# A decoder layer on one core: the first pooling group and a value projection change places with an attention block

## The chip, the cores and the metric

The kernel runs on one core of a Trainium2 chip. The metric is the device time of one launch in microseconds (us); the median of three runs is given. A profile is one further execution, recorded by the hardware profiler, whose span is measured from its first to its last instruction.

The engines are named as in the profile: PE (TensorE, matrix multiply; PEld is its weight load), DVE (VectorE), ACT (ScalarE), POOL (GpSimd) and SP (SyncE, which here only issues transfers).

## The reference

One decoder layer over 1024 tokens of width 1024, in float32. Cut to what matters here:

```python
z = h @ w_in                     # columns: [pool group 512 | q 512 | k 128 | v 128]
y_pool = pool_mixer(u_pool, w_pool, pool_scale)   # causal mean over 2, 4, 8, 16 tokens
                                                  # minus the token, then a 128x128 map
                                                  # per group of 128 channels, a scale per channel
y_attn = sliding_window_attention(q, k, v, sinks) # window 128, 8 query heads, 2 key heads,
                                                  # ALiBi bias, one sink per head
mix = concat(y_pool, y_attn) @ w_out
h = layer_norm(alpha * h + mix)
h = layer_norm(alpha * h + relu(h @ w_ff1)**2 @ w_ff2)
h = h + sigmoid(h @ w_gate + b) * (p @ w_ple)
```

## The kernel before

Each float32 operand is split into a high part, which ACT writes (`high`, L101), and a low part, which DVE computes as operand minus high part (`low`, L106). A product is then three matmuls on PE, high by high, high by low and low by high (`mm3`, L116 to L118).

The part that matters here is the first quarter of the kernel. The tokens are worked in two halves of 512 (`t` is 0 or 1). `z_tile(c, t)` loads one 128-column block of `w_in` (1024 rows), splits it, and issues 24 matmuls of 128x512 into one accumulator. Blocks 0 and 1 are the keys and values, 2 to 5 the queries, 6 to 9 the four pooling groups.

`attention(n)` (n is 0 to 7) treats 128 queries against 256 keys, for two key heads. For each key head it makes two score tiles `s` of 128x2x256 (L298, L299), adds bias and takes the row maximum on DVE (L302, one instruction for each of the two query heads of a tile, followed by a short read of its accumulator), exponentiates on ACT (L309), scales by the reciprocal on DVE (L313, L315), transposes on PE (L322), splits (L101, L106 on `pp`) and multiplies by the values (L327, L328) into `av`; L330 on ACT and L331 on DVE add its two halves.

`pool_group(gi, t, o)` takes the accumulator `o` of a pooling block: ACT copies it to a row (L358), POOL forms the window sums by doubling (L366) and mends the first tokens (L374, L375, first half only), DVE subtracts the token (L369), `tmp` takes the split result, three matmuls apply the 128x128 map into a new accumulator `y`, and ACT (L103) and DVE (L385) write the scaled and split result.

PSUM is shared out as follows. Accumulators `mm` have three buffers, score tiles `s` two, transposed tiles `pt` two, `av` one. `tmp` has one buffer. `out_left`, which multiplies the mixer's output by the left half of `w_out`, needs four accumulators and takes the fourth from the two `s` buffers:

```python
os = [acc_ps() for _ in range(3)]
os.append(ps.tile([P, HALF], F32, tag="s", bufs=2, name=nm("s")))
```

The order of the instructions on each engine is not the order of the program. The framework runs its own timeline model over the program (`schedule_with_timeline_sim=True`) and emits, on each engine, what the model finds ready, in program order where several are ready. A buffer is handed to the next tile of its kind once its last reader is done. So a change in the program's order moves instructions on all engines, up to where the two orders meet again. The weight loads of `z_tile` are issued on SP; a `st` buffer (two) is free for the next load when DVE has written the low part of the one before.

Before the change, `pooling(n)` keeps two pooling blocks projected and closes n groups; the sequence around the change is at L500 to L513.

Of the kernel before, what the change touches and what calls it, by code (L numbers as in the profile page):

```python
# [70 lines left out]
def layer(ctx, tc, xT, x, pT, w_in, w_pool, pscale, sinks, w_out, ln1, w1, w2, ln2, w_ple, w_gate, bgate, bias, rcount, out):  # L71
# [11 lines left out]
    def big(shape, dt=F32R):  # L83
        return sb.tile(shape, dt, tag="c", bufs=6, name=nm("c"))
# [7 lines left out]
    def stage(shape):  # L92
        return sb.tile(shape, F32, tag="st", bufs=2, name=nm("st"))
# [5 lines left out]
    def high(dst, src, scale=None):  # L99
        if scale is None:  # L100
            nc.scalar.copy(out=dst, in_=src)  # L101
        else:
            nc.scalar.mul(out=dst, in_=src, mul=scale)  # L103

    def low(eng, dst, src, hi):
        return eng.tensor_tensor(out=dst, in0=src, in1=hi.bitcast(F32), op=ALU.subtract)  # L106

    def load_split(dst_h, dst_l, src, shape, eng, st=None, queue=None):
        st = stage(shape) if st is None else st
        load = (queue or nc.sync).dma_start(out=st, in_=src)  # L110
        high(dst_h, st)
        low(eng, dst_l, st, dst_h)
        return load

    def mm3(o, ah, al, bh, bl, first, last, more=False):
        nc.tensor.matmul(o, ah, bh, start=first, stop=False, skip_group_check=more)  # L116
        nc.tensor.matmul(o, ah, bl, start=False, stop=False, skip_group_check=more)  # L117
        nc.tensor.matmul(o, al, bh, start=False, stop=last, skip_group_check=more)  # L118
# [30 lines left out]
    def keep(shape, dt=F32R):  # L149
        return pa.tile(shape, dt, tag="k", bufs=3, name=nm("k"))  # L150

    def tmp(shape, dt=F32):
        return pa.tile(shape, dt, tag="tmp", bufs=1, name=nm("tmp"))

    def row(shape, dt=F32):
        return pa.tile(shape, dt, tag="h", bufs=6, name=nm("h"))
# [14 lines left out]
    def acc_ps():  # L171
        return ps.tile([P, HALF], F32, tag="mm", bufs=3, name=nm("mm"))

    def tr_ps():
        return ps.tile([P, 4, P], F32, tag="pt", bufs=2, name=nm("pt"))
# [9 lines left out]
    def z_mm(o, w, t, k):  # L185
        xk = xs[t][k // 4]
        mm3(o, w[:, 0, k, :], w[:, 1, k, :], xk[:, 0, k % 4, :], xk[:, 1, k % 4, :], k == 0, k == NK - 1)
# [3 lines left out]
    def z_tile(c, t, home=None):  # L191
        w = (home or wt)([P, 2, NK, P])
        loads.append(load_split(w[:, 0], w[:, 1], w_in[c], [P, NK, P], nc.vector))
        o = acc_ps()
        for k in range(NK):
            z_mm(o, w, t, k)
        return o
# [45 lines left out]
    def values(t, o):  # L243
        if t == 0:
            VV[0] = keep([P, NT, 2, 2, HD])
        vt = row([P, HALF])
        copied = nc.scalar.copy(out=vt, in_=o)
        pv = tr_ps()
        for b in range(4):
            nc.tensor.transpose(pv[:, b, :], vt[:, b * P : (b + 1) * P], ident)  # L250
        v4 = pv.rearrange("p b (g d) -> p b g d", g=2)
        dst = VV[0][:, 4 * t : 4 * t + 4]
        for g in range(2):
            high(dst[:, :, g, 0, :], v4[:, :, g, :])
            low(nc.vector, dst[:, :, g, 1, :], v4[:, :, g, :], dst[:, :, g, 0, :])
        return copied
# [5 lines left out]
    def queries(t, half):  # L262
        for j in (2 * half, 2 * half + 1):
            o = first[2] if t == j == 0 else z_tile(2 + j, t, big if t == 0 and j == 1 else None)
            q = nat([P, 2, HALF], F32R)
            QQ[t][j] = q
            for i in range(2):
                r = slice(i * HD, (i + 1) * HD)
                sc = HD ** -0.5 / SLOPES[2 * j + i]
                high(q[0:HD, i, :], o[r, :], sc)  # L270
                nc.vector.scalar_tensor_tensor(
                    out=q[HD:P, i, :], in0=o[r, :], scalar=sc, in1=q[0:HD, i, :].bitcast(F32),
                    op0=ALU.mult, op1=ALU.subtract,
                )
# [69 lines left out]
    steps = [(gi, t) for t in range(2) for gi in (3, 2, 1, 0)]  # L344
    ahead = []

    def pooling(n):
        for _ in range(n):
            while steps and len(ahead) < 2:
                gi, t = steps.pop(0)  # L350
                ahead.append((gi, t, z_tile(6 + gi, t)))
            pool_group(*ahead.pop(0))

    def pool_group(gi, t, o):
        win = WINDOWS[gi]
        u = row([P, PAD + HALF])
        nc.gpsimd.tensor_copy(out=u[:, 0:PAD], in_=halo[:, gi, :])
        nc.scalar.copy(out=u[:, PAD:], in_=o)  # L358
        if t == 0:
            nc.gpsimd.tensor_copy(out=halo[:, gi, :], in_=u[:, HALF : HALF + PAD])  # L360
        sums = [row([P, PAD + HALF]) for _ in range(2)]
        cur, a, side = 1, u, 0
        while cur < win:
            d0 = 2 * cur - 1
            b = sums[side]
            nc.gpsimd.tensor_tensor(out=b[:, d0:], in0=a[:, d0:], in1=a[:, d0 - cur : PAD + HALF - cur], op=ALU.add)  # L366
            a, side, cur = b, 1 - side, 2 * cur
        dd = sums[side][:, PAD:]
        nc.vector.scalar_tensor_tensor(  # L369
            out=dd, in0=a[:, PAD:], scalar=1.0 / win, in1=u[:, PAD:], op0=ALU.mult, op1=ALU.subtract  # L370
        )
        if t == 0:
            f = win - 1
            nc.gpsimd.tensor_tensor(out=dd[:, 0:f], in0=a[:, PAD : PAD + f], in1=rc[:, 0:f], op=ALU.mult)  # L374
            nc.gpsimd.tensor_tensor(out=dd[:, 0:f], in0=dd[:, 0:f], in1=u[:, PAD : PAD + f], op=ALU.subtract)  # L375
        dT = tmp([P, 2, HALF], F32R)
        high(dT[:, 0], dd)
        low(nc.vector, dT[:, 1], dd, dT[:, 0])
        y = acc_ps()
        mm3(y, wp[:, 0, gi, :], wp[:, 1, gi, :], dT[:, 0], dT[:, 1], True, True)  # L380
        if mixP[t] is None:
            mixP[t] = big([P, 2, 4, HALF])
        m = mixP[t]
        high(m[:, 0, gi, :], y, psc[:, gi : gi + 1])
        nc.vector.scalar_tensor_tensor(  # L385
            out=m[:, 1, gi, :], in0=y, scalar=psc[:, gi : gi + 1], in1=m[:, 0, gi, :].bitcast(F32),
            op0=ALU.mult, op1=ALU.subtract,
        )
# [71 lines left out]
    def out_left(t, staging, eng, room=None):  # L460
        blocks = range(4 * t, 4 * t + 4)
        os = [acc_ps() for _ in range(3)]
        os.append(ps.tile([P, HALF], F32, tag="s", bufs=2, name=nm("s")))
        for k in range(NK):
            if k % 2 == 0:
                w = room[:, k // 2 - 2] if room is not None and k > 3 else wt([P, 2, 2, HALF])
                out_load(w, 0, k // 2, staging(), eng)
            for n in blocks:
                out_mm(os[n % 4], n, k, w)
        return os  # L470
# [29 lines left out]
    keys(1, z_tile(0, 1))  # L500
    attention(2)
    queries(1, 1)
    pooling(1)
    attention(3)
    values(1, z_tile(1, 1))
    pooling(1)
    attention(4)
    pooling(2)
    attention(5)
    pooling(2)  # L510
    attention(6)
    pooling(2)
    left = out_left(0, lambda: stage([P, 2, HALF]), nc.vector)  # L513
    with tc.issue_after(loads[-1].ins):
        residual_load(0)
# [639 lines left out]
```

## Time and profile before

| | |
|---|---|
| median of three runs | 984.94 us (984.05 to 985.39) |
| the profiled execution, its own time | 984.01 us |
| its span, first to last instruction | 982.2 us, granted TensorE clock 1.000 |
| PE busy in the span | 973.8 us of 982.2 |
| DVE, ACT, POOL busy | 750.4, 470.6, 129.5 us |

The profiled execution's own time is 1.8 us more than its span, and 0.93 us below the median of the runs. In the profile, "idle before" an instruction is the time in which its engine did nothing, and the arrow names what it waited for. In a timeline row stand the start, the duration, the engine, the line, the operation, the tile written and those read, and the shapes; rows of one group are merged, so that "x4" is four instructions one after another.

### The profile page before, as it was taken

The numbers are of one execution on the slowest core, as the hardware profiler recorded it, in microseconds if no ns is written. First come the engines' busy times: TensorE is split into PE (matmuls) and PEld (weight loads), VectorE is DVE, ScalarE is ACT, GpSimd is POOL, SyncE is SP. The second block draws the span as 40 slices with busy tenths as digits, with TensorE's granted clock in tenths as the row PEclk, the third lists the DMA queues.
The fourth block names the chain that finished last, engine by engine and source line by source line (L and its number), as shares of the span: only waits on it lengthen the run. The fifth ranks groups of instructions, "written<-read, shape, count | busy, mean of one in ns | idle before, by whom it ended". The sixth has DMA issues, their size and how long they took to land.

```text
span 982.2 us, 12301 instructions
## 1 busy us (share of the span) xinstructions
PE 973.8 (99%) x4474; PEld 809.3 (82%) x4474; DVE 750.4 (76%) x1188; ACT 470.6 (48%) x749; POOL 129.5 (13%) x185
## 2 busy tenths in 40 slices
PE   9999999999999999999999999999999999999998
PEld 7888887888888888888888888888888888878887
DVE  5798888895868876867547666888657699799895
ACT  5676666543475443434444344443434354554341
POOL 0013552020010000110000000100011111203210
PEclk9999999999999999999999999999999999999999
DMA  6512142623152544896264794675788866762741
GB/s 220 183 65 86 44 150 75 219 82 115 69 198 103 197 150 159 298 324 242 78 245 172 278 322 149 150 243 194 207 217 190 223 158 225 252 193 77 257 148 55
DMA packets 48188, 172.13 MB, mean 175 GB/s; under 512 B 6016, under 2 KB 7168, under 8 KB 45312
## 3 DMA queue, kind: packets, MB, share of 16 engines
q1 hardware_dynamic: 35584, 130.05, 38.6%
q0 software_dynamic: 10960, 36.71, 14.6%
q10 hardware_dynamic: 1584, 4.59, 1.2%
q8 instruction: 35, 0.57, 0.2%
q14 instruction: 25, 0.20, 0.1%
HBM read 138.82 MB, written 32.51 MB: 174 GB/s over the span
## 4 chain that ended last, share of the span: by engine, by line
PE 94%; DVE 2%; DMA 2%; issue 1%; ACT 1%; DVEq 0%
PE f L117 21%; PE f L118 21%; PE f L116 21%; PE mm L116 8%; PE mm L118 8%; PE mm L117 8%; DMA ws<-in_w_gate 2%; PE pt L322 1%; PE s L299 1%; PE s L298 1%; PE av L328 1%; PE av L327 1%; DVE w L106 0%; PE s L116 0%; ACT c L101 0%
## 5 line engine op out<-in xcount | busy, mean ns | idle before, releaser
L117 PE MATMUL f<-x,w 128*128 128x512 f32 x448 | 174.0, 389 | 0.4 <-DVE x L106 0.4
L118 PE MATMUL f<-x,w 128*128 128x512 f32 x448 | 173.9, 389 | 0.0
L116 PE MATMUL f<-c,ws 128*128 128x512 f32 (+1 forms) x420 | 162.5, 387 | 0.0
L117 PE MATMUL f<-c,ws 128*128 128x512 f32 (+1 forms) x420 | 162.5, 387 | 0.0
L118 PE MATMUL f<-c,ws 128*128 128x512 f32 (+1 forms) x420 | 161.3, 387 | 0.0
L116 PE MATMUL f<-x,w 128*128 128x512 f32 x448 | 147.1, 389 | 0.1
L101 ACT CAST w<-st 128x1024 fp32r<-128x1024 f32 (+2 forms) x66 | 65.6, 999 | 100.2 <-issue 57.9
L106 DVE TENSOR_TENSOR w<-st,w 128x1024 fp32r<-128x1024 f32 (+2 forms) x66 | 77.5, 1177 | 46.9 <-ACT w L101 46.8
L117 PEld LDWEIGHTS f<-x,w 128*128 128x128 f32 x448 | 84.1, 188 | 18.8 <-DVE x L106 1.1
L116 PEld LDWEIGHTS f<-x,w 128*128 128x128 f32 x448 | 84.0, 188 | 17.9 <-ACT x L101 0.5
L118 PEld LDWEIGHTS f<-x,w 128*128 128x128 f32 x448 | 84.1, 188 | 17.3
L118 PEld LDWEIGHTS f<-c,ws 128*128 128x128 f32 x420 | 78.9, 188 | 16.5 <-DVE ws L106 0.4
L117 PEld LDWEIGHTS f<-c,ws 128*128 128x128 f32 x420 | 78.9, 188 | 16.0
L116 PEld LDWEIGHTS f<-c,ws 128*128 128x128 f32 x420 | 78.9, 188 | 16.0
L106 DVE TENSOR_TENSOR x<-ws,x 128x1024 fp32r<-128x1024 f32 x54 | 65.8, 1219 | 1.5 <-ACT x L101 1.5
L101 ACT CAST ws<-w 128x512 fp32r<-128x512 f32 x60 | 36.9, 622 | 52.0 <-PE f L118 26.5
L106 DVE TENSOR_TENSOR ws<-w,ws 128x512 fp32r<-128x512 f32 x60 | 41.2, 690 | 25.3 <-ACT ws L101 24.6
L101 ACT CAST x<-ws 128x1024 fp32r<-128x1024 f32 x54 | 56.6, 1048 | 7.4 <-DMA ws<-gT 4.0
L101 ACT CAST ws<-st 128x512 fp32r<-128x512 f32 x48 | 29.8, 620 | 62.2 <-DVE st L121 30.8
L116 PE MATMUL mm<-c,w 128*128 128x512 f32 x144 | 56.4, 396 | 0.3 <-ACT w L101 0.3
L118 PE MATMUL mm<-c,w 128*128 128x512 f32 x144 | 56.6, 394 | 0.0
L117 PE MATMUL mm<-c,w 128*128 128x512 f32 x144 | 56.4, 393 | 0.0
(236 smaller groups left out, 1905.5 us busy)
## 6 DMA issues: line engine op xcount, KB each, us to landing
ws<-in_w SPq DMA_DIRECT2D x70, 512.0 KB, 3.8
w<-in_w SPq DMA_DIRECT2D x16, 1024.0 KB, 5.4
c<-fd SPq DMA_DIRECT2D x6, 2048.0 KB, 8.6
fd<-n POOLq DMA_DIRECT2D x20, 512.0 KB, 4.3
ws<-in_w POOLq DMA_DIRECT2D x20, 512.0 KB, 7.6
st<-in_w_in SPq DMA_DIRECT2D x17, 512.0 KB, 3.4
ws<-in_w_gate SPq DMA_DIRECT2D x16, 512.0 KB, 4.6
w<-in_w SPq DMA_DIRECT2D x10, 512.0 KB, 4.0
```

What stands on the lines that cost most here:

```text
L101: nc.scalar.copy(out=dst, in_=src)
L106: return eng.tensor_tensor(out=dst, in0=src, in1=hi.bitcast(F32), op=ALU.subtract)
L116: nc.tensor.matmul(o, ah, bh, start=first, stop=False, skip_group_check=more)
L117: nc.tensor.matmul(o, ah, bl, start=False, stop=False, skip_group_check=more)
L118: nc.tensor.matmul(o, al, bh, start=False, stop=last, skip_group_check=more)
L298: nc.tensor.matmul(s[:, i, dst], ql, kt[:, 0, g, kk : kk + kn], start=True, stop=False)
L299: nc.tensor.matmul(s[:, i, dst], ql, kt[:, 1, g, kk : kk + kn], start=False, stop=True)
L322: nc.tensor.transpose(pt[:, i, :], e[:, i, kb * P : (kb + 1) * P], ident)
L327: nc.tensor.matmul(av, VV[0][:, blk, g], pp[:, 0], start=(kb == lo), stop=False)
L328: nc.tensor.matmul(av, VV[0][:, blk, g], pp[:, 1], start=False, stop=(kb == 1))
```

## The change

The function `pooling` is replaced by `project`, which only projects the next pooling block; the groups are closed by explicit calls of `pool_group`. The sequence of projections and groups is the same as before from `attention(4)` on. In front of it two things change places: the first pooling group (window 16, first half of the tokens) was closed ahead of `attention(3)` and is closed after it, and the projection of the second half's values, `z_tile(1, 1)`, was behind that group and stands ahead of it, while the rest of `values` follows it.

```diff
-    def pooling(n):
-        for _ in range(n):
-            while steps and len(ahead) < 2:
-                gi, t = steps.pop(0)
-                ahead.append((gi, t, z_tile(6 + gi, t)))
-            pool_group(*ahead.pop(0))
+    def project():
+        gi, t = steps.pop(0)
+        ahead.append((gi, t, z_tile(6 + gi, t)))
...
     attention(2)
     queries(1, 1)
-    pooling(1)
+    project()
+    project()
     attention(3)
-    values(1, z_tile(1, 1))
-    pooling(1)
+    zv = z_tile(1, 1)
+    pool_group(*ahead.pop(0))
+    values(1, zv)
+    project()
+    pool_group(*ahead.pop(0))
     attention(4)
-    pooling(2)
+    project()
+    pool_group(*ahead.pop(0))
+    project()
+    pool_group(*ahead.pop(0))
...
```

No instruction of the computation is added or removed; lines below the function stand three lower in the changed file (L369 is L366 there, L385 is L382). The orders of the two kernels differ on PE from the middle of `attention(3)`'s scores to the start of the second half's `out_left`, and are the same before and after.

On PE, at the end of the scores of `attention(3)`, there stood in a row before (`pt` transposes of attention 2; `s_1001`, `s_1044` and `s_1051` the second, third and fourth score tile of attention 3; `mm_984` the first pooling group's map; `mm_1099` the values' projection):

```order
L322 MATMUL pt_823<-ident,e_786 128x128 x4
L299 MATMUL s_1001<-k_283,n_344 128x256
L298 MATMUL s_1044<-k_283,n_395 128x256
L299 MATMUL s_1044<-k_283,n_395 128x256
L298 MATMUL s_1044<-k_283,n_395 128x256
L299 MATMUL s_1044<-k_283,n_395 128x256
L298 MATMUL s_1051<-k_283,n_430 128x256
L299 MATMUL s_1051<-k_283,n_430 128x256
L298 MATMUL s_1051<-k_283,n_430 128x256
L299 MATMUL s_1051<-k_283,n_430 128x256
L116 MATMUL mm_984<-tmp_981,wp 128x512
L116 MATMUL mm_1099<-c_136,w_1094 128x512
```

and now, at the same place (`s_978` is the second score tile, `mm_1076` the values' projection):

```order
L322 MATMUL pt_823<-ident,e_786 128x128 x4
L299 MATMUL s_978<-k_283,n_344 128x256
L298 MATMUL s_978<-k_283,n_344 128x256
L299 MATMUL s_978<-k_283,n_344 128x256
L116 MATMUL mm_1076<-c_136,w_1071 128x512
L117 MATMUL mm_1076<-c_136,w_1071 128x512
```

The eleventh of those projection matmuls is the first row here; behind it comes the third score tile, `s_1021`, and then the projection again:

```order
L117 MATMUL mm_1076<-c_136,w_1071 128x512
L298 MATMUL s_1021<-k_283,n_395 128x256
L299 MATMUL s_1021<-k_283,n_395 128x256
L298 MATMUL s_1021<-k_283,n_395 128x256
L299 MATMUL s_1021<-k_283,n_395 128x256
L118 MATMUL mm_1076<-c_136,w_1071 128x512
```

Eleven matmuls of the values' projection now stand between the second and the third score tile, and thirteen more between the third and the fourth, which was directly behind the third.

On DVE, in the same stretch, the first pooling group's subtraction stood ahead of the weight split `w_1135`, and both between the two score tiles' maxima; before:

```order
L302 ISA e_992,sm_993<-s_994,nd,sink_sb 128x256
L302 ISA sm_993 128x1
L369 SCALAR_TENSOR_TENSOR h_972<-h_973,h_968 128x512
L106 TENSOR_TENSOR w_1135<-st_1136,w_1135 128x1024
L302 ISA e_992,sm_993<-s_1001,nd,sink_sb 128x256
```

and now:

```order
L302 ISA e_969,sm_970<-s_971,nd,sink_sb 128x256
L302 ISA sm_970 128x1
L106 TENSOR_TENSOR w_1135<-st_1136,w_1135 128x1024
L366 SCALAR_TENSOR_TENSOR h_1105<-h_1106,h_1101 128x512
L331 TENSOR_TENSOR y_735<-av_762,yl_783 64x512
L302 ISA e_969,sm_970<-s_978,nd,sink_sb 128x256
```

L369 (now L366) and `w_1135` have changed places, and L331 of attention 2 now stands ahead of the second tile's maxima too.

On DVE, ahead of the left half of the first `out_left` (its fourth accumulator, `s_1775` on PE, takes the buffer of the score tile `s_1659`, which the L302 rows at the end read), there stood before:

```order
L369 SCALAR_TENSOR_TENSOR h_1742<-h_1743,h_1739 128x512
L313 RECIPROCAL sm_1608<-sm_1608 128x4
L385 SCALAR_TENSOR_TENSOR c_1555<-mm_1551,psc,c_1555 128x512
L315 TENSOR_SCALAR e_1607<-e_1607,sm_1608 128x256 x4
L385 SCALAR_TENSOR_TENSOR c_1555<-mm_1600,psc,c_1555 128x512
L106 TENSOR_TENSOR tmp_1747<-h_1742,tmp_1747 128x512
L106 TENSOR_TENSOR w_1805<-st_1806,w_1805 128x1024
L302 ISA e_1657,sm_1658<-s_1659,nd,sink_sb 128x256
```

and now:

```order
L382 SCALAR_TENSOR_TENSOR c_1555<-mm_1551,psc,c_1555 128x512
L302 ISA e_1607,sm_1608<-s_1616,nd,sink_sb 128x256
L302 ISA sm_1608 128x1
L106 TENSOR_TENSOR tmp_1597<-h_1592,tmp_1597 128x512
L302 ISA e_1607,sm_1608<-s_1616,nd,sink_sb 128x256
L302 ISA sm_1608 128x1
L106 TENSOR_TENSOR w_1776<-st_1777,w_1776 128x1024
L302 ISA e_1657,sm_1658<-s_1659,nd,sink_sb 128x256
```

The maxima of `s_1659` now stand ahead of `h_1742`, the scaling of `e_1607`, the result of `mm_1600`, `tmp_1747` and `w_1805`, all of which come behind them; `w_1805`, the second quarter of `w_out`, has moved 13 rows further back, behind the maxima of the next score tile and the scaling of `e_1657`.

More of the change, by code (lines that the diff above doesn't have):

```diff
@@ L502, in layer @@
     queries(1, 1)
-    pooling(1)
+    project()
+    project()
     attention(3)
-    values(1, z_tile(1, 1))
-    pooling(1)
+    zv = z_tile(1, 1)
[3 more added lines that the diff above has]
+    pool_group(*ahead.pop(0))
     attention(4)
-    pooling(2)
+    project()
+    pool_group(*ahead.pop(0))
+    project()
+    pool_group(*ahead.pop(0))
     attention(5)
-    pooling(2)
+    project()
+    pool_group(*ahead.pop(0))
+    project()
+    pool_group(*ahead.pop(0))
     attention(6)
-    pooling(2)
+    project()
+    pool_group(*ahead.pop(0))
+    pool_group(*ahead.pop(0))
     left = out_left(0, lambda: stage([P, 2, HALF]), nc.vector)
```

## The prediction

> **What bounds the kernel now.** I read the page's busy shares first, then the chain that ended last, then the busy time by stage, PE's waits, and the timeline at each wait.
>
> ```profile
> PE 973.8 (99%) x4474; PEld 809.3 (82%) x4474; DVE 750.4 (76%) x1188; ACT 470.6 (48%) x749; POOL 129.5 (13%) x185
> PE 94%; DVE 2%; DMA 2%; issue 1%; ACT 1%; DVEq 0%
> ```
>
> The first row gives each engine's busy time, the second the shares of the chain. PE carries 94% of it; a change that adds no PE work can gain only PE's idle time. Where that lies (columns: stretch, its length, busy time of PE, PEld, DVE, ACT and POOL, granted clock, DMA share, GB/s):
>
> ```profile
> 5.00:75.00 70.00, 69.68 (x338) 58.47 (x338) 56.71 (x123) 47.43 (x100) 6.71 (x8) 1.00 0.45 152
> 75.00:130.00 55.00, 54.10 (x294) 46.17 (x293) 43.88 (x107) 37.63 (x85) 24.35 (x36) 1.00 0.28 98
> 130.00:180.00 50.00, 48.79 (x253) 40.76 (x252) 43.90 (x105) 34.17 (x82) 18.31 (x21) 1.00 0.29 95
> 180.00:260.00 80.00, 80.00 (x376) 66.58 (x375) 61.74 (x121) 33.03 (x46) 10.32 (x9) 1.00 0.36 122
> 700.00:875.00 175.00, 174.51 (x768) 143.25 (x766) 136.95 (x156) 78.48 (x82) 23.16 (x32) 1.00 0.79 210
> 875.00:982.20 107.20, 103.11 (x482) 86.42 (x482) 91.24 (x149) 38.24 (x51) 16.99 (x29) 1.00 0.41 137
> ```
>
> The change reorders instructions between about 90 and 212 us. There PE is idle 0.90 us in one stretch and 1.21 us in another; the last stretch's 4.1 us are the output's tail behind the last matmul, which nothing here touches. PE's waits name the two:
>
> ```profile
> PE s L116 <- DVE sm L302: 1.2, 1, 1.2
> PE s L298 <- DVE sm L302: 0.9, 1, 0.9
> PE f L117 <- DVE x L106: 0.4, 1, 0.4
> ```
>
> Both waits are for a score buffer: PE may not write the next tile into one of the two `s` buffers until DVE's L302 has read the old one. They lie here (start, duration, engine, operation; idle time in brackets):
>
> ```profile
> 92.35 0.28 PE L298 MATMUL s<-k,n 128*128 128x256 f32 x1
> 92.47 0.28 PE L299 MATMUL s<-k,n 128*128 128x256 f32 x1
> 92.70 0.28 PE L299 MATMUL s<-k,n 128*128 128x256 f32 x1
> 93.88 0.39 PE L298 MATMUL s<-k,n 128*128 128x256 f32 x1 [0.90 <-DVE sm L302]
> 155.85 0.50 PE L117 MATMUL mm<-tmp,wp 128*128 128x512 f32 x1
> 156.18 0.40 PE L118 MATMUL mm<-tmp,wp 128*128 128x512 f32 x1
> 157.79 0.50 PE L116 MATMUL s<-w,c 128*128 128x512 f32 x1 [1.21 <-DVE sm L302]
> ```
>
> Starts are the better measure, since matmuls overlap. Score matmuls follow each other at 0.12 us (92.35 to 92.47), so the first wait costs 93.88 - 92.70 - 0.12 = 1.06 us. The pitch of 128x512 matmuls comes from a run of 18:
>
> ```profile
> 94.74 0.39 PE L116 MATMUL mm<-c,w 128*128 128x512 f32 x1
> 98.59 0.39 PE L118 MATMUL mm<-c,w 128*128 128x512 f32 x1
> ```
>
> 17 steps in 3.85 us, 0.227 us each; the second wait costs 157.79 - 156.18 - 0.23 = 1.38 us. What DVE did meanwhile:
>
> ```profile
> 91.19 0.69 DVE L369 SCALAR_TENSOR_TENSOR h<-h,h 128x512 f32<-128x512 f32 x1
> 91.79 1.22 DVE L106 TENSOR_TENSOR w<-st,w 128x1024 fp32r<-128x1024 f32 x1
> 92.93 0.48 DVE L302 CUSTOM_DVE_ANT_0 e<-s,nd,sink_sb 128x256 f32<-128x256 f32 x1
> 93.73 0.68 DVE L331 TENSOR_TENSOR y<-av,yl 64x512 f32<-64x512 f32 x1
> 151.19 0.68 DVE L369 SCALAR_TENSOR_TENSOR h<-h,h 128x512 f32<-128x512 f32 x1
> 151.89 0.75 DVE L385 SCALAR_TENSOR_TENSOR c<-mm,psc,c 128x512 fp32r<-128x512 f32 x1
> 152.56 1.41 DVE L315 TENSOR_SCALAR e<-e,sm 128x256 f32<-128x256 f32 x4
> 153.89 0.74 DVE L385 SCALAR_TENSOR_TENSOR c<-mm,psc,c 128x512 fp32r<-128x512 f32 x1
> 154.55 1.25 DVE L106 TENSOR_TENSOR tmp<-h,tmp 128x512 fp32r<-128x512 f32 x1
> 155.72 1.21 DVE L106 TENSOR_TENSOR w<-st,w 128x1024 fp32r<-128x1024 f32 x1
> 156.85 0.47 DVE L302 CUSTOM_DVE_ANT_0 e<-s,nd,sink_sb 128x256 f32<-128x256 f32 x1
> ```
>
> In both cases DVE works off pooling and weight pieces that stand ahead of the maxima PE waits for. That order is what moves.
>
> **The change, part by part.** Nothing is added or removed: the moved group's POOL adds, its ACT copy and casts, its DVE pieces and its three matmuls are the same, and PE's work is the same to the instruction. So the sum has only waits in it.
>
> *First wait.* PE finishes the second score tile at about 92.3 us as before. DVE still has a weight split (1.14 from start to start), L369 (0.60), and now L331 (0.68) ahead of that tile's maxima, and reads them by 91.2 + 2.4 + 0.8 = 94.4 us. PE does not ask then: 11 matmuls, the third tile (into the first tile's buffer, read by 91.2) and 13 more stand ahead of the fourth tile, 24 x 0.227 + 0.46 = 5.9 us, which it reaches at 98.2. The wait goes with 3.8 us to spare: -1.06 us. What is delayed is the chain behind the third tile, whose softmax starts 2.5 us later; its transposes stand behind all of attention 3's scores and 24 matmuls in both orders, so I put that at nothing.
>
> *Second wait.* Before, the buffer was free at about 157.65 (156.85 and two maxima at 0.4). Now h_1742 with a reciprocal, the scaling, one L385, tmp_1747 and w_1805 stand behind these maxima: by the starts above 0.70 + 1.33 + 0.66 + 1.17 + 1.13 = 5.0 us less ahead of them. So the buffer is free at 152.7 even if DVE reclaims no idle time. PE asked at 156.18 + 0.23 = 156.41; now it asks 1.06 us earlier for the first wait, and some 0.45 earlier because three matmuls of a pooling map went behind and one of attention came ahead: 154.9. The wait goes with 2.2 us to spare: -1.38 us.
>
> *What is late next.* w_1805, the second quarter of `w_out`. Behind it before, and ahead of it now, are four maxima, L331, two `pp` splits and one scaling of four, about 1.6 + 0.7 + 1.2 + 1.1 = 4.6 us; before it was written by 156.85, so by 161.5 if DVE ran as solidly as it did. PE needs it about 2.44 us earlier than it would, behind 16 rows that now come ahead of it (four of attention 0.9, eight transposes 0.9, four scores 0.46): I get 159.3. So this step costs between 0 and 2.2 us. DVE's idle stretches ahead of it say how much it can reclaim:
>
> ```profile
> 121.44 1.52 DVE L106 TENSOR_TENSOR w<-st,w 128x1024 fp32r<-128x1024 f32 x1 [0.48 <-ACT w L101]
> 129.44 0.48 DVE L302 CUSTOM_DVE_ANT_0 e<-s,nd,sink_sb 128x256 f32<-128x256 f32 x1 [1.99 <-PE pt L322]
> 137.01 0.69 DVE L106 TENSOR_TENSOR tmp<-h,tmp 128x512 fp32r<-128x512 f32 x1 [0.74 <-ACT tmp L101]
> 145.67 0.69 DVE L106 TENSOR_TENSOR tmp<-h,tmp 128x512 fp32r<-128x512 f32 x1 [0.76 <-ACT tmp L101]
> ```
>
> They sum to 3.97 us, most of it waiting for PE, which is now earlier. Following DVE's new order row by row with these durations, I find w_1805 written at about 157.7, 1.6 us ahead of need. I take 0 and keep 2.2 as the other end.
>
> *The rest of the stretch.* Walking PE's, DVE's, ACT's and POOL's new orders the same way, the tightest other places have 1.3 to 2 us to spare (the fifth pooling group's `tmp`, the scaling of attention 5). On SP the `w_in` loads keep their order; four rows of `w_out` and of x change places behind the left half. Two rows for that and for what comes later:
>
> ```profile
> ACT c L101 <- DMA st<-in_w_out: 4.3, 4, 1.6
> 829.47 1.06 ACT L101 CAST x<-ws 128x1024 fp32r<-128x1024 f32 x1 [3.47 <-PE f L118]
> ```
>
> ACT already waits for these `w_out` loads, four times, 1.6 us at most, and PE does not: its matmuls of the left half cover it. A load late by as much again would take that cover; price 0, at most 1.6 us. From the second `out_left` on the orders are equal and PE is solid to 869 us, so an earlier PE stays earlier. The 0.4 us wait of `f` there ends a chain of casts and loads that starts with the second row, which waits for a matmul; it moves along.
>
> One row speaks of DVE against POOL:
>
> ```profile
> 138.78 3.80 POOL L366 TENSOR_TENSOR h<-h 128x527 f32<-128x527 f32 x2 [1.02 <-ACT h L358]
> 141.85 2.46 DVE L315 TENSOR_SCALAR e<-e,sm 128x256 f32<-128x256 f32 x4
> 162.32 1.14 DVE L315 TENSOR_SCALAR e<-e,sm 128x256 f32<-128x256 f32 x4
> ```
>
> Beside POOL's adds the scaling took 2.46 us, without them 1.14, and two adds took 3.80. A collision costs DVE 1.3 us. The same number of adds and scalings meet in the same stretch; I price a change in their meetings from -1.3 to +1.3 us on DVE, value 0, and nothing on PE while 1.5 us are to spare. The Trainium skill ("SBUF — State Buffer", Who interferes with whom) has it that the two engines share one pair of ports as an exclusive lock, so that the later one blocks for a whole instruction; these rows agree in kind. By that rule alone the moved group's adds could hold DVE once more at each scaling they now meet, and the time would be that of the first rival below.
>
> *Sum.* -1.06 - 1.38 = -2.44 us. Against the profiled execution: 984.01 - 2.44 = 981.6; the median of the runs was 0.93 above it, so 984.94 - 2.44 = 982.5 us.
>
> **The rivals.** 0.2% is 2.0 us, about what a measurement of this kernel can tell from no change.
>
> *A part comes back.* The first wait goes, but DVE, which is busy 43.9 of 50 us between 130 and 180, is late with w_1805 or with one scaling because of one more collision: 1.3 us of 2.44 returned, 983.8. For it speak the solid DVE rows from 146 to 158; against it the 3.97 us idle.
>
> *Nothing gained.* The model placed the old order without seeing the two waits, so it can place new ones as large: w_1805's full 2.2 us gives 984.7. Against it: in my walk each place has over 1 us to spare.
>
> *Slower.* The left half's fourth accumulator holds one of the two `s` buffers from its first matmul to the end of the left half. Before, three of attention 7's four score tiles had to share the other buffer in that time, and the fourth came after; now all four come within it. Each then waits for two maxima of the one before. If DVE is over 4 us behind PE there (my walk has it 4 us ahead at the second tile), each pays about what the second wait paid: 4 x 1.38 = 5.5 us, less 2.44 gained, +3.1 or 988.0.
>
> **How the numbers follow.** Forecast as summed 0.54; a part back 0.25; nothing gained 0.11; slower 0.10. The predicted time is the first's, 982.5. Its own range is 981.7 to 983.3 (the bounds of small waits, and 0.7 us by which runs differ). The range goes on to the second and third cases: 981.5 to 985.3. For faster by over 0.2% the time must be under 982.97, so the first case falls there mostly, and a little to the other side: faster 0.50, within 0.2% 0.40, slower 0.10.
>
> **What would show it.** In the new profile PE should have no idle row of 0.9 before an L298 near 93 us, the third score tile should start near 94.8, and no L116 on `s` should wait near 155. PE idle in the stretch from 75 to 180 should be under 0.5 us instead of 2.1, busy time of PE the same, and the span 979.8. A wait of PE for DVE's `w` L106 near 159 would show the first rival or the second by its size; several waits for L302 between 157 and 175 the last. I would be wrong altogether if DVE's order lets a piece I took as early, such as `tmp`, hold PE where before it did not.

## The result, and the profile after

The changed kernel takes 982.76 us (median of 12 runs, 981.70 to 983.47) beside 984.75 us of the kernel before (12 runs, 983.59 to 986.25): a ratio of 0.9979, interval 0.9970 to 0.9987, or 2.0 us less. The profiled execution of it took 982.35 us with a span of 980.6. Its page, busy shares and chain:

```profile
PE 974.0 (99%) x4474; PEld 808.8 (82%) x4474; DVE 752.7 (77%) x1188; ACT 470.5 (48%) x749; POOL 126.5 (13%) x185
PE 90%; DVE 6%; DMA 2%; issue 1%; ACT 1%; ACTq 0%; DVEq 0%
```

PE's work is the same. DVE's share of the chain rose from 2% to 6%, but that says little by itself: a second profile of the old order (values_behind_group below) has 5%. What belongs to the change is a piece from 138.4 to 161.4 us, where the chain, followed back from a new wait, leaves PE and runs along DVE and ACT. The stretches and PE's waits:

```profile
75.00:130.00 55.00, 55.00 (x298) 46.91 (x297) 47.40 (x113) 38.71 (x89) 24.09 (x37) 1.00 0.25 89
130.00:180.00 50.00, 49.31 (x256) 40.89 (x255) 45.37 (x108) 35.34 (x84) 18.87 (x20) 1.00 0.34 117
```

```profile
PE s L117 <- DVE w L106: 0.5, 1, 0.5
PE av L328 <- DVE pp L106: 0.2, 1, 0.2
```

PE's idle time from 75 to 180 us fell from 2.11 to 0.69 us. Both waits for L302 are gone from the list, and two small ones for DVE's pieces have come. At the place of the first wait (timeline; the last matmul of the second score tile, the first of the third and of the fourth):

```profile
91.78 0.28 PE L299 MATMUL s<-k,n 128*128 128x256 f32 x1
...
94.42 0.28 PE L298 MATMUL s<-k,n 128*128 128x256 f32 x1
...
98.09 0.28 PE L298 MATMUL s<-k,n 128*128 128x256 f32 x1
```

Neither tile has idle time in front. At the place of the second, the fourth accumulator starts at the pitch of 0.23 us:

```profile
154.08 0.39 PE L118 MATMUL mm<-c,w 128*128 128x512 f32 x1
154.31 0.39 PE L116 MATMUL s<-w,c 128*128 128x512 f32 x1
```

What came instead lies 4 us later:

```profile
158.41 0.40 PE L116 MATMUL s<-w,c 128*128 128x512 f32 x1
159.34 0.50 PE L117 MATMUL s<-w,c 128*128 128x512 f32 x1 [0.53 <-DVE w L106]
...
160.75 0.47 PE L327 MATMUL av<-pp,k 128*128 128x512 f32 x1
161.38 0.50 PE L328 MATMUL av<-pp,k 128*128 128x512 f32 x1 [0.16 <-DVE pp L106]
```

From start to start PE lost 159.34 - 158.41 - 0.23 = 0.70 us waiting for the low part of `w_1805`, and 161.38 - 160.75 - 0.23 = 0.40 us for the low part of a `pp`. DVE and POOL at that time:

```profile
148.18 1.50 DVE L106 TENSOR_TENSOR w<-st,w 128x1024 fp32r<-128x1024 f32 x1
...
152.88 1.12 DVE L315 TENSOR_SCALAR e<-e,sm 128x256 f32<-128x256 f32 x4
...
156.19 1.96 DVE L315 TENSOR_SCALAR e<-e,sm 128x256 f32<-128x256 f32 x4
158.07 1.21 DVE L106 TENSOR_TENSOR w<-st,w 128x1024 fp32r<-128x1024 f32 x1
```

```profile
156.15 1.07 POOL L363 TENSOR_TENSOR h<-h 128x527 f32<-128x527 f32 x1 [4.34 <-DVE sm L313]
```

The scaling ahead of `w_1805` took 1.96 us beside POOL's add and 1.12 three microseconds earlier, without one.

**A finer measure than the run time.** From the eight transposes of attention 1 at 63 us to the first transposes into `av` at 233 us lies all that the change moves. The rows that bound it, of the kernel before and of the changed one:

```profile
63.10 1.03 PE L322 MATMUL pt<-ident,e 128*128 128x128 f32 x8
...
234.52 0.60 PE L444 MATMUL av<-ident,n 128*128 128x128 f32 x4
```

```profile
62.66 1.03 PE L322 MATMUL pt<-ident,e 128*128 128x128 f32 x8
...
232.79 0.60 PE L441 MATMUL av<-ident,n 128*128 128x128 f32 x4
```

That is 171.42 us before and 170.13 after: 1.29 us less, of 1.6 in the span. The same two rows of every profile taken in this study:

| kernel | start | stretch | rest of the span |
|---|---|---|---|
| before | 63.10 | 171.42 | 747.68 |
| values_behind_group (the order of before) | 64.01 | 171.46 | 747.23 |
| values_ahead_only | 62.83 | 171.79 | 747.78 |
| changed kernel | 62.66 | 170.13 | 747.81 |
| after_again (unaltered) | 63.51 | 170.15 | 746.94 |
| double_add | 62.83 | 170.71 | 747.76 |
| sum_on_dve | 63.29 | 169.92 | 747.19 |
| window2_direct | 63.04 | 169.33 | 747.63 |
| weights_first_window2 | 62.64 | 169.34 | 747.32 |
| weights_first | 63.12 | 169.01 | 748.27 |
| weights_first_again (unaltered) | 63.73 | 169.02 | 746.35 |
| no_sums | 63.05 | 168.59 | 746.36 |

Three orders were profiled twice, and their stretches repeat to 0.01, 0.02 and 0.04 us, while the start scatters over 1.4 us and the rest over 1.9 us whatever the kernel. The scatter of the runs is that of the start and the rest. So below the stretch carries the verdicts, and the ratio (to runs of the kernel before that were made beside each experiment) is given with it.

### The profile page after: what moved, and what is told of

The parts are those of the page before. It is cut to its first block, busy times and chain, and to the rows that moved or that the text cites. A ratio compares the mean times of both kernels' runs of the same rounds, so it can differ in the third digit from the quotient of the medians.

```text
span 980.6 us, 12293 instructions
## 1 busy us (share of the span) xinstructions
PE 974.0 (99%) x4474; PEld 808.8 (82%) x4474; DVE 752.7 (77%) x1188; ACT 470.5 (48%) x749; POOL 126.5 (13%) x185
## 4 chain that ended last, share of the span: by engine, by line
PE 90%; DVE 6%; DMA 2%; issue 1%; ACT 1%; ACTq 0%; DVEq 0%
PE f L117 21%; PE f L118 21%; PE f L116 20%; PE mm L116 8%; PE mm L117 8%; PE mm L118 8%; DMA ws<-in_w_gate 1%; DVE w L106 1%; PE pt L322 1%; DVE x L106 1%; PE s L299 1%; PE s L298 1%; PE av L328 1%; DVE pre L121 1%; PE av L327 1%
## 5 line engine op out<-in xcount | busy, mean ns | idle before, releaser
L118 PE MATMUL f<-c,ws 128*128 128x512 f32 (+1 forms) x420 | 161.4, 387 | 0.0
L118 PEld LDWEIGHTS f<-c,ws 128*128 128x128 f32 x420 | 78.9, 188 | 16.3 <-DVE ws L106 0.4
```

## The experiments

**One half of the change alone.** In values_behind_group the projection is moved and the group stays:

```diff
     project()
     project()
-    attention(3)
-    zv = z_tile(1, 1)
     pool_group(*ahead.pop(0))
+    zv = z_tile(1, 1)
+    attention(3)
     values(1, zv)
```

> One half of the change alone: the projection of the second half's values stands ahead of attention 3, but the first pooling group stays in its old place ahead of it. The scheduler gives every engine the rows of the kernel before, in the same order, so this is a second look at that program. Theory (both waits belong to that order): the ratio is 1.000 within 0.0007, and the profile shows both waits for a score buffer again, about 0.9 us before an L298 near 93 us and 1.2 us before an L116 on s near 157.8. Rival (part of what the two profiles differ by is the start of that one execution, where the changed kernel's rows stood 0.45 us earlier already at 63 us, ahead of any moved row): this profile stands nearer to the changed kernel's at 63 us, by up to 0.45 us.

983.9 us, ratio 0.9998 (0.9989 to 1.0007). Both waits are there again, to 0.01 us (idle 0.90 and 1.21 in the kernel before):

```profile
94.78 0.39 PE L298 MATMUL s<-k,n 128*128 128x256 f32 x1 [0.89 <-DVE sm L302]
...
158.72 0.51 PE L116 MATMUL s<-w,c 128*128 128x512 f32 x1 [1.21 <-DVE sm L302]
```

So the waits belong to the order and not to an execution. The rival on the start isn't borne out in its direction: the transposes stood at 64.01, 0.9 us later than before, not earlier. But it shows that the changed profile's lead of 0.44 us at that row is within what the same program does by itself. Half of the change is no change: the scheduler gives the old order back on every engine, so this run is a second look at the kernel before and no test of the projection alone.

In values_ahead_only the projection comes ahead of the group, and both ahead of attention 3:

```diff
     project()
     project()
-    attention(3)
     zv = z_tile(1, 1)
     pool_group(*ahead.pop(0))
+    attention(3)
     values(1, zv)
```

> The other way to make half of the change: the projection of the values stands ahead of the first pooling group, and both stay ahead of attention 3. Here all 24 of its matmuls come before attention 3's scores, and on DVE w_1805 stands behind the two maxima of s_1659, as in the changed kernel, but also behind pp_1488 and pp_1498. Theory (each wait goes when DVE's pieces ahead of the maxima go): no wait of about 1 us near 93 us, and the second wait shrinks from 1.38 by 1.13 (w_1805) less 0.65 (pp_1488), to about 0.9; so 1.06 + 0.5 = 1.6 us less than the kernel before, 983.2 us, ratio 0.9984. Rival (the moved group does it, its DVE piece and its three matmuls behind attention 3): both waits stay, ratio 1.000.

984.04 us, ratio 1.0001 (0.9992 to 1.0010), stretch 171.79: nothing gained. The theory had the old waits right and the time wrong: both are gone, even the 0.9 us that it had left of the second. In their place PE waits for the first half of a pooling `tmp`, which ACT casts late, and three shorter times. Its list of waits, and the largest in the timeline:

```profile
PE mm L116 <- ACT tmp L101: 0.9, 1, 0.9
...
PE s L298 <- DVE sm L302: 0.4, 2, 0.2
PE av L327 <- DVE y L331: 0.2, 1, 0.2
```

```profile
160.19 0.40 PE L118 MATMUL s<-w,c 128*128 128x512 f32 x1
161.50 0.50 PE L116 MATMUL mm<-tmp,wp 128*128 128x512 f32 x1 [0.91 <-ACT tmp L101]
```

161.50 - 160.19 - 0.23 = 1.08 us. My sum had ended at the waits that I knew, and priced at nothing what is late next. That is the step which failed in the prediction too.

**Is it POOL's add that makes w_1805 late?** First the add taken off POOL, then doubled. sum_on_dve:

```diff
-            nc.gpsimd.tensor_tensor(out=b[:, d0:], ...)
+            (nc.vector if t == 1 and gi == 0 else nc.gpsimd).tensor_tensor(out=b[:, d0:], ...)
```

> The changed kernel with the one window sum of the last pooling group (window 2, second half) added on DVE and not on POOL. PE's order is the same up to well behind 159 us; on DVE the sum stands between the scaling of attention 6 and w_1805. In the changed kernel POOL's add at 156.15 (1.07 us) lies beside that scaling, which takes 1.96 us and not the 1.12 of one alone, and w_1805 is written so late that PE waits 0.70 us for it and 0.40 for pp. Theory (POOL holds DVE up): the scaling takes 1.1 to 1.3 us; w_1805 comes 0.84 earlier for that and 0.6 later for the sum, so PE's wait for it is 0.4 to 0.5 us; time 982.0 to 982.7. Rival (DVE is late by the order and amount of its own work, the scaling is long for another reason): the scaling still takes about 1.9 us, w_1805 comes 0.6 later, PE's wait for it grows to 1.3 us, time 983.3.

981.43 us, less than both figures expected; ratio 0.9973 (0.9961 to 0.9984), stretch 169.92. The waits decide here. On DVE:

```profile
156.81 1.14 DVE L315 TENSOR_SCALAR e<-e,sm 128x256 f32<-128x256 f32 x4
157.87 0.70 DVE L363 TENSOR_TENSOR h<-h 128x527 f32<-128x527 f32 x1
```

On PE:

```profile
159.05 0.40 PE L116 MATMUL s<-w,c 128*128 128x512 f32 x1
159.76 0.51 PE L117 MATMUL s<-w,c 128*128 128x512 f32 x1 [0.31 <-DVE w L106]
```

The scaling is back to 1.14, and the wait is 0.71 - 0.23 = 0.48 us, as the theory had it and not the rival's 1.3. The stretch gained only 0.21 us, since the sum now stands on DVE ahead of `pp` too, for which PE waits 161.80 - 161.02 - 0.23 = 0.55 us:

```profile
161.02 0.39 PE L327 MATMUL av<-pp,k 128*128 128x512 f32 x1
161.80 0.50 PE L328 MATMUL av<-pp,k 128*128 128x512 f32 x1 [0.38 <-DVE pp L106]
```

double_add:

```diff
-            nc.gpsimd.tensor_tensor(out=b[:, d0:], ...)
+            for _ in range(2 if (t, gi) == (1, 0) else 1): nc.gpsimd.tensor_tensor(out=b[:, d0:], ...)
```

> The changed kernel with that one window sum done twice on POOL (the same values again). On DVE the rows up to w_1805 keep their order; behind it the last group's pieces come later, and on PE its map does. Theory (POOL holds DVE up): the second add of about 1.07 us lies beside the end of the scaling and w_1805, which together take 0.5 to 1.1 us longer; PE's wait for w_1805 grows from 0.70 to between 1.2 and 1.8 us, time 983.3 to 983.9. Rival (POOL's adds cost DVE nothing there): scaling and w_1805 take 1.96 and 1.21 us as in the changed kernel, PE's wait stays at 0.70, time 982.8.

983.1 us, between the theory's 983.3 and the rival's 982.8; ratio 0.9989 (0.9980 to 0.9998), stretch 170.71. On DVE, and then on PE:

```profile
156.36 2.84 DVE L315 TENSOR_SCALAR e<-e,sm 128x256 f32<-128x256 f32 x4
159.12 1.21 DVE L106 TENSOR_TENSOR w<-st,w 128x1024 fp32r<-128x1024 f32 x1
```

```profile
158.59 0.40 PE L116 MATMUL s<-w,c 128*128 128x512 f32 x1
160.38 0.50 PE L117 MATMUL s<-w,c 128*128 128x512 f32 x1 [1.40 <-DVE w L106]
```

The wait is 1.79 - 0.23 = 1.56 us. So with no, one and two adds the same scaling takes 1.14, 1.96 and 2.84 us, and PE waits for `w_1805` 0.48 (with the sum of 0.6 us on DVE in between), 0.70 and 1.56 us. POOL's add is shown to be a cause.

**The changed kernel once more.**

> The changed kernel once more, unaltered, to see how far its own runs and a second profile agree. The profiles so far, taken from the first transposes of attention 1 (63 us) to the first transposes into av at 233 us, give it 171.42 - 170.13 = 1.29 us less than before in that stretch, and nothing later. Theory (that stretch is the whole effect): a ratio between 0.9980 and 0.9990, and 170.1 us within 0.1 for the stretch. Rival (the first comparison's 2.0 us are right and part of the gain lies outside it): 0.9975 to 0.9980.

981.34 us, ratio 0.9982 (0.9974 to 0.9991), stretch 170.15. This agrees with the theory, but the interval reaches past the rival's figures too. The stretch repeats to 0.02 us. Whether some more of the gain lies outside it stays open: both comparisons show about 2 us, and the rest of the span, 747.81 and 746.94 in this order, 747.68 and 747.23 in the old one, scatters too much to tell.

**Without the add and without a sum.** window2_direct uses that a mean of two less the token is half the difference to the one before:

```diff
+        half = (gi, t) == (0, 1)
+        if half:
+            nc.gpsimd.tensor_scalar(out=u[:, 0:PAD], in0=halo[:, gi, :], scalar1=0.5, scalar2=None, op0=ALU.mult)
+            nc.scalar.mul(out=u[:, PAD:], in_=o, mul=0.5)
...
-        while cur < win:
+        while cur < win and not half:
...
+        if half:
+            add(dd, u[:, PAD - 1 : PAD + HALF - 1], u[:, PAD:], ALU.subtract)
```

> The changed kernel with the last pooling group's window of 2 formed without a sum: ACT halves the row as it copies it, and DVE's one subtraction takes the token from its predecessor, so POOL's 1.07 us add is gone and DVE has no instruction more. PE's order is the same; on DVE the subtraction (0.6 us) comes ahead of w_1805 instead of behind it. Theory (POOL's add holds the scaling up by 0.82 us): scaling 1.12 to 1.14 us; w_1805 0.82 earlier less 0.6, PE's wait for it about 0.5 instead of 0.70; everything behind it on DVE 0.8 earlier, so the wait of 0.40 for pp goes; the stretch from 63 to 233 us 169.5, ratio 0.9982 of before. Rival (the wait for pp comes from PE being earlier, not from DVE): it stays at 0.4 and the stretch is 169.9.

981.68 us, ratio 0.9982 (0.9973 to 0.9991), stretch 169.33 (169.5 expected). PE:

```profile
158.79 0.40 PE L116 MATMUL s<-w,c 128*128 128x512 f32 x1
159.49 0.50 PE L117 MATMUL s<-w,c 128*128 128x512 f32 x1 [0.30 <-DVE w L106]
```

The scaling took 1.15 us, the wait for `w_1805` is 0.47 us, and that for `pp` is gone: it was DVE's lateness too.

**The order of the pieces.** weights_first loads and splits the first two quarters of `w_out` ahead of the last group (`out_weights` does for one quarter what stood in `out_left`, which takes the two as they are):

```diff
     pool_group(*ahead.pop(0))
+    early = [out_weights(k, lambda: stage([P, 2, HALF]), nc.vector) for k in (0, 2)]
     pool_group(*ahead.pop(0))
-    left = out_left(0, lambda: stage([P, 2, HALF]), nc.vector)
+    left = out_left(0, lambda: stage([P, 2, HALF]), nc.vector, None, early)
```

> The changed kernel with the load and split of the first two quarters of w_out written ahead of the last pooling group in the program. On PE the fourth pp matmul and the second four transposes come ahead of a run of weights' matmuls; on DVE w_1805 keeps its place, and the two pp splits come ahead of the last group's subtraction instead of behind it. POOL's add stays. Theory (each wait is DVE's rows ahead of the piece waited for): the scaling still takes 1.96 us and the wait for w_1805 stays at 0.70; the pp pieces come 0.6 us earlier, so the wait of 0.40 for them goes, if nothing waits for the later subtraction; stretch from 63 to 233 us about 169.7, ratio 0.9984. Rival (the order of the program sets DVE's lateness as a whole): the wait for w_1805 goes too, 169.0.

981.4 us, ratio 0.9981 (0.9973 to 0.9990), stretch 169.01. The rival's figure, by the theory's mechanism: I had looked at PE's and DVE's order and not at ACT's. ACT casts `w_1805` ahead of the row's copy, so POOL's add starts 0.90 us behind the scaling, where it started 0.04 ahead of it in the changed kernel, and holds none of its four instructions:

```profile
155.89 1.04 ACT L101 CAST w<-st 128x1024 fp32r<-128x1024 f32 x1
156.83 0.57 ACT L355 COPY h<-mm 128x512 f32<-128x512 f32 x1
```

```profile
156.64 1.14 DVE L315 TENSOR_SCALAR e<-e,sm 128x256 f32<-128x256 f32 x4
157.70 1.22 DVE L106 TENSOR_TENSOR w<-st,w 128x1024 fp32r<-128x1024 f32 x1
```

```profile
157.54 2.30 POOL L363 TENSOR_TENSOR h<-h 128x527 f32<-128x527 f32 x1 [5.29 <-ACT h L355]
```

Now it is POOL that is held up: its add takes 2.30 us, 1.07 and the 1.22 of DVE's split, which lost nothing. PE waits for neither `w_1805` nor the first `pp`.

With both edits:

> Both edits together: no POOL add in the last group, and the split w_1805 ahead of that group's subtraction on DVE. Theory (POOL's add is what made w_1805 late; without it the forecast's own walk holds): w_1805 is written 0.82 us earlier than in the changed kernel and PE does not wait for it (0.70 gone); pp comes 0.8 earlier while PE asks 0.7 earlier, so 0.3 us of 0.40 stay at most; the stretch from 63 to 233 us is 169.1 (171.42 of before less the 2.44 forecast makes 169.0), ratio 0.9976 of before. Rival (DVE is late for its amount of work): w_1805 is still waited for, 0.3 us or more, and the stretch is 169.6 or more.

981.09 us, ratio 0.9975 (0.9966 to 0.9984), stretch 169.34:

```profile
158.40 0.40 PE L116 MATMUL s<-w,c 128*128 128x512 f32 x1
158.63 0.39 PE L117 MATMUL s<-w,c 128*128 128x512 f32 x1
...
159.90 0.47 PE L327 MATMUL av<-pp,k 128*128 128x512 f32 x1
160.53 0.50 PE L328 MATMUL av<-pp,k 128*128 128x512 f32 x1 [0.16 <-DVE pp L106]
```

No wait for `w_1805`, as the theory says; but the 0.40 for `pp` stayed whole, where I expected 0.3 at most, because that split stands behind the group's subtraction on DVE; in weights_first, where the first `pp` split stands ahead of it, PE does not wait. The stretch missed 169.1 by that.

**The shortest one again.**

> The kernel with the first two quarters of w_out loaded and split ahead of the last pooling group, once more and unaltered, since its stretch from 63 to 233 us (169.01) was the shortest seen, though the last expectation had it wrong: ACT casts w_1805 ahead of the row's copy there, so POOL's add starts 0.7 us later, behind the scaling, which took 1.14 us. Theory (the stretch repeats, the rest of the span does not): 169.0 within 0.05, a ratio of 0.9975 to 0.9983 of before. Rival (the stretch was a chance of that execution): 169.5 or more.

980.79 us, ratio 0.9972 (0.9963 to 0.9981), stretch 169.02. It repeats. This version is 1.1 us shorter in the stretch than the changed kernel; the run times (0.9981 and 0.9972 beside 0.9979 and 0.9982) don't separate the two.

**All window sums left out.**

> The changed kernel without any of POOL's window sums: each pooling group takes the row itself where the sum stood, so 20 adds of POOL are left out and the rest stays; the engines' orders shift between 90 and 212 us. DVE has the same instructions. In the changed kernel DVE is busy 47.40 and 45.37 us in the stretches from 75 to 130 and from 130 to 180 us. Theory (POOL's adds hold DVE up): by the excess of its rows over the time of the same instruction alone, 5.0 us in the scalings and about 2 in the rest, DVE's busy time there falls from 92.8 to between 85 and 88 us, and no scaling of four takes over 1.5 us but beside another POOL instruction. Rival (the long rows have another cause): it stays within 1 us of 92.8.

One run, 979.8 us; stretch 168.59. PE is idle nowhere from 75 to 180 us here. DVE is busy 87.5 us in that time, within the 85 to 88 expected, where it was 92.8; but work has also moved out of the window (40 scalings lie in it instead of 44, and from 180 to 260 us DVE is busy 64.21 us where it was 60.40). Over the whole kernel, with the same 1188 instructions, DVE's time falls only from 752.7 to 750.2 us:

```profile
PE 972.2 (99%) x4474; PEld 808.7 (83%) x4474; DVE 750.2 (77%) x1188; ACT 469.7 (48%) x749; POOL 103.0 (11%) x165
```

The scalings, in the changed kernel and here (groups of DVE from 75 to 180 us, busy and mean of one):

```profile
L315 DVE TENSOR_SCALAR e<-e,sm 128x256 f32<-128x256 f32 x44 | 17.5, 456 | 0.2
```

```profile
L315 DVE TENSOR_SCALAR e<-e,sm 128x256 f32<-128x256 f32 x40 | 11.7, 350 | 0.2
```

350 ns each, where they were 456: no long scaling is left. Over the whole kernel the 56 scalings of this shape take 16.3 us here and 21.0 in the changed kernel. But the order has moved too, and sums are not all that holds DVE up. The scaling at 143.22 us of the changed kernel (2.19 us) lay beside a split of `c` on POOL (143.70, 1.29 us). Here three splits of `tmp` on DVE, 0.67 to 0.69 us alone, take 1.43 to 1.73 us beside such splits; the first of them:

```profile
87.59 1.73 DVE L106 TENSOR_TENSOR tmp<-h,tmp 128x512 fp32r<-128x512 f32 x1
```

```profile
87.48 1.29 POOL L106 TENSOR_TENSOR c<-y,c 128x512 fp32r<-128x512 f32 x1 [1.25 <-ACT c L101]
```

So the long scalings come from meetings with POOL's instructions, its sums and its splits of `c`. The 2 us that the theory expected from the rest of DVE's rows did not come.

## Why the prediction was right, and where it was wrong

*First wait, -1.06 us:* right. The third score tile started at 94.42 (forecast 94.8) and the fourth at 98.09 (98.2), without idle time.

*Second wait, -1.38 us:* right. PE asked at 154.31 (154.9) and got the buffer at once.

*What is late next, 0:* wrong, and this is the step that failed. I named the place, the tile and the bound (0 to 2.2 us), and took the lower end from my walk along DVE: `w_1805` written at 157.7, 1.6 us ahead of need. It was written at 158.07 + 1.21 = 159.28 and cost 0.70 us, and the `pp` behind it 0.40 more. Of the 1.6 us between walk and trace, 0.84 is the scaling at 156.19 (1.96 for 1.12), and 0.3 the split at 148.18 (1.50 for 1.21). The rest of some 0.5 I did not trace, and it is more like 0.9, since the changed profile already stands 0.44 us earlier at 63 us. The prediction had counted the scaling among the rows ahead of `w_1805` at 1.1 us, the time of one alone. It also called the 3.97 us of idle time mostly waits for PE; only 1.99 of them are, and the others are waits for ACT.

*POOL against DVE, -1.3 to +1.3 on DVE, 0 on PE:* wrong in size and in consequence. "The same number of adds and scalings meet" did not hold: DVE's busy time rose by 2.3 us for the same 1188 instructions (750.4 before and 750.5 in values_behind_group, 752.7 and 752.6 in the two profiles of the changed kernel). The scalings more than account for it, with 18.1 us over the whole kernel before and 21.0 after. Before, the longest row of four took 2.46 us and two took 1.41; now the rows at 143.22 and 156.19 take 2.19 and 1.96, and two more are long:

```profile
102.75 3.00 DVE L315 TENSOR_SCALAR e<-e,sm 128x256 f32<-128x256 f32 x4
132.45 2.26 DVE L315 TENSOR_SCALAR e<-e,sm 128x256 f32<-128x256 f32 x4
```

The one at 156.19 is shown to reach PE; the one at 143.22 lies on the chain too, and what it costs was not measured. I let the term cost PE nothing "while 1.5 us are to spare", which the same walk had found. The two terms were not independent: one collision took half of the spare time of the other.

*The rest:* right as far as can be seen. No other wait appeared between 75 and 260 us, and the rest of the span did not shorten by more than it scatters (747.68 and 747.23 in the old order, 747.81 and 746.94 in the new).

*Sum:* 2.44 forecast; in the stretch 2.44 - 0.70 - 0.40 = 1.34 worked out from the waits, 1.29 measured. So what happened is the first rival: the two waits went, and "one more collision" took back 1.1 us, of the 1.3 that I gave it. The two terms of the forecast hold where nothing comes behind them: in weights_first, where PE waits for neither `w_1805` nor the first `pp`, the stretch is 171.42 - 169.01 = 2.41 us shorter than before. The median came out at 982.76, 0.26 from the forecast and under the line of 982.97, because the first comparison shows 2.0 us less, of which the stretch accounts for 1.29; a second one gave 0.9982. The difference lies inside the intervals. So the forecast's closeness is luck: its sum is nearly twice the gain that the stretch shows, and the 0.7 us that bring the median near it are located nowhere. Of the signs that I listed, PE idle from 75 to 180 us is 0.69 (under 0.5 forecast), the span 980.6 (979.8), and the wait for `w` near 159 named the first rival, as the list said it would.

*The two other rivals* did not occur here. But "nothing gained" is what the other half of the change did (values_ahead_only): new waits as large as the old.

## What to carry to other kernels

When a wait is removed, walk on to the piece that is late next, and walk it twice: once with the durations of rows that stood alone and once with those that met a neighbour; price what the second walk loses, even where the first one has more to spare than one collision costs (here 1.6 us beside 0.84). Read the orders of all engines, ACT's and POOL's too, since one cast that changes places with a copy on ACT can decide whether DVE and POOL meet. Where a change acts within one stretch, measure from a fixed row ahead of it to a fixed row behind it: here that repeats to 0.04 us, while the run times of the same program scatter over 2 us and more.

## What the runs showed of the hardware

How an add on POOL and an instruction on DVE share time was known in kind from the profile before, but not which of the two pays. Where POOL's add came as a scaling began (156.15 against 156.19) the scaling waited: 1.14, 1.96 and 2.84 us with no, one and two adds, 0.82 and 0.88 us for each of about 1.07. Each add holds one of the four instructions: with one add the first took 1.17 us and the other three 0.34 each. Where DVE was already in a row of instructions (weights_first: the scaling from 156.64 to 157.78, the split from 157.70), DVE lost nothing, and the add, whose row begins at 157.54, took 2.30 us. A split on POOL does the same as an add: the scaling at 143.22 and the `tmp` split at 87.59 were held beside one.

The Trainium skill ("SBUF — State Buffer", Who interferes with whom) says that a DVE instruction in a mode that uses two ports, which it says `tensor_scalar` can enter, contends with POOL for a shared pair of ports, that whoever issues first gets the pair for the whole instruction, and that the other fully blocks. The rows above agree that one of the two is held for a whole instruction, in both directions. They don't settle who goes first: the row of the split in weights_first begins 0.16 us behind that of the add, and the split went first all the same. The Trainium skill adds, in the same section, that an operation of two tensors blocks with POOL's reads when both its inputs lie in SBUF: the split of 1.22 us that held the add is one of these.
